# Two PSUM banks of the common ring per attention unit, in place of one ring bank and a third of a shared bank

## The chip, the cores and the metric

The kernel runs on one core of one Trainium2 chip. The metric is the device time of one execution in microseconds (us), the median of several runs. Five engines work side by side, each on its own list of instructions in order: TensorE (PE in the profile; its weight loads are listed as PEld), VectorE (DVE), ScalarE (ACT), GpSimd (POOL) and SyncE (SP), which here only issues DMAs. PE writes its products into PSUM, which this kernel divides into eight banks of 512 fp32 columns by 128 partitions; DVE and ACT read them from there.

## The reference

Two layers over 2048 tokens of width 1024. What matters here is group B, attention with 8 query heads of width 64 and 2 key/value heads:

```python
for l in range(DEPTH):                      # DEPTH = 2
    h = rmsnorm(x, pre_g[l])
    u_a, v_a, g_a, q, k, v, g_b = jnp.split(h @ w_in[l], idx, axis=-1)
    y_a = gmlp_group(u_a, v_a, ...) * silu(g_a)
    y_b = gqa_axial_attention(q, k, v, ...) * silu(g_b)   # softmax(q k^T) v, all 2048 keys
    x = x + rmsnorm(concat(y_a, y_b) @ w_out[l], post_g[l])
```

## The kernel before

**Stages.** Each layer has a projection stage (`Project.run`, the products with `w_in`, the gating of group A, the rotary embedding) and an attention stage (`attend`). In the profiled execution attention takes about 617 to 1372 us in the first layer and 1981 to 2726 us in the second.

**Units and steps.** Attention is cut into 32 units per layer, `units[u]`: one query head and one block of 512 queries, which are four pieces of 128 (`TPG` = 4). The loop at L1097 walks over steps `k`; a unit has 16 steps, one for each 128 keys. A step does, in this order: on PE two matmuls for the scores `sp` of its 128 keys against the 512 queries (L1106, L1107); on ACT two exponentials of them, an fp16 one into `p_hi` (called `p_parts` in the profile) and an fp32 one into `p_f`; on POOL, and on DVE in 15% of the steps, the difference `p_lo` of the two (also `p_parts`). Then come the jobs that a table `later` holds for this step: for most steps one `pmax` matmul on PE with a row maximum `mx` on DVE, which prepare a later unit; then some matmuls `pout` of the output projection that fill in (`pop_fill`). Last, PE multiplies the probabilities of the step three back (`LAG` = 3) with the values.

**The product with the values.** For each of the four query pieces j there are two matmuls into `s.av[j]` (L1137, L1139): `p_hi` with 129 columns (64 of the value's low part, 64 of its high part, one column of ones for the denominator) and `p_lo` with the last 65 of these. The eight matmuls of a step add to the same 4 x 129 columns over all 16 steps. 4 x 129 = 516 columns are more than one bank's 512. So pieces 0 to 2 lie in a bank `po` from the common ring (`ps_t`, L73, seven banks), and piece 3 in one third of a fixed eighth bank `po_3` (L165), `u % 3` saying which third.

**The end of a unit.** After a unit's last step, `finish` (L722) enters its closing jobs into `later`. In the following step, `evac`: for each of the two banks an ACT copy of the low parts to `o_pair` and a small DVE operation that makes `rden` of the denominators. One step later, `add`: for each bank a DVE addition of the high parts. Then, another step later, `gate` and `mul` (DVE), and after every second unit a transposition (`trans`, `split`). Since the jobs of `later` stand ahead of the product with the values within a step, a unit's `evac` is recorded just ahead of the first product of the next unit, and its `add` ahead of the second one.

**What sets the order.** The operations of this stage are recorded through `Pinned` (L86), which keeps each engine's instructions in the order in which the program writes them. The framework that builds the program adds the waits: it orders any two accesses to one bank of one tile by different engines, whichever columns they touch. It also deals out the ring: a new tile gets a bank whose previous tile is finished, and its first writer waits for the last reader of that previous tile. All other PSUM tiles (`sp`, `pmax`, `pout`, `t2`, `py`, and in projection `pp`, `pt`, `sq`) come from the same ring.

Of the kernel before, what the change touches and what calls it, by code (L numbers as in the profile page):

```python
# [9 lines left out]
F32 = mybir.dt.float32  # L10
# [9 lines left out]
P = 128  # L20
D = 1024
ND = D // P
GRP = 512
TPG = GRP // P
# [6 lines left out]
VN = 2 * HD + 1  # L31
# [9 lines left out]
def encoder(ctx: ExitStack, tc, x, w_in, w_out, pre_g, post_g, ln_a_g, ln_a_b,  # L41
# [16 lines left out]
    psum = ctx.enter_context(tc.tile_pool(name="psum", bufs=1, space=PSUM))  # L58
# [8 lines left out]
    def f_t(name, n=GRP, dt=F32):  # L67
        return fp.tile([P, n], dt, name=name, tag="f")
# [2 lines left out]
        return rowp.tile(list(shape), dt, name=name, tag="row")  # L71

    def ps_t(name):  # L73
        return psum.tile([P, GRP], F32, name=name, tag="ps", bufs=7)

    class Pinned:

# [66 lines left out]
    class Background:  # L144
# [16 lines left out]
        def flush(self):  # L161
            while self.jobs:
                self.jobs.pop(0)[1]()

    po_3 = psum.tile([P, GRP], F32, name="po_3")  # L165

    bg = Background()
    PASSES = ((0, 0), (0, 1), (1, 0))
# [467 lines left out]
    T_DELAY = 9  # L636
    VA_DELAY = 9
    LAG = 3
    AV_BANKED = 3
    N_HI = 8  # L640
    N_F = 4
    N_LO = 8
# [4 lines left out]
    def attend(l, kv, nxt):  # L647

        k_st, k_lo, _, v16 = kv
# [23 lines left out]
        def at(k, f):  # L673
            later.setdefault(k, []).append(f)
# [47 lines left out]
        def finish(u, k):  # L722

            qb, h = units[u]
            side = h % 2
            s, pr = state[u], pairs[u // 2]
            r = slice(side * HD, (side + 1) * HD)

            def evac():
                if side == 0:  # L730
                    pr.o = f_t("o_pair").rearrange("p (t e) -> p t e", t=TPG)
                s.rd = small.tile([P, TPG], F32, name="rden")
                for b, js in s.banks:
                    ACT.copy(pr.o[:, js, r], b[:, :, 0:HD])
                    DVE.tensor_scalar(s.rd[:, js], b[:, :, 2 * HD], layers[l].two, None, ALU.mult)

            def add():
                for b, js in s.banks:
                    DVE.tensor_tensor(pr.o[:, js, r], b[:, :, HD:2 * HD], pr.o[:, js, r], ALU.add)

            def gate():
                DVE.reciprocal(s.rd, s.rd)
                gv = pr.gb[:, :, r]
                DVE.tensor_tensor(gv, gv, s.rd.unsqueeze(2).broadcast_to([P, TPG, HD]), ALU.mult)

            def mul():
                DVE.tensor_tensor(pr.o[:, :, r], pr.o[:, :, r], pr.gb[:, :, r], ALU.mult)

            def trans():
                pr.py = ps_t("py")  # L750
                for j in range(TPG):
                    PE.transpose(pr.py[:, j * P:(j + 1) * P], pr.o[:, j], ident)

            def split():
                y_hi = f_t("y_hi", dt=F32R)
                y_lo = f_t("y_lo", dt=F32R)
                ACT.copy(y_hi, pr.py)
                DVE.tensor_tensor(y_lo, pr.py, y_hi.bitcast(F32), ALU.subtract)
                if (qb, h) == units[-1]:
                    last_y.extend([y_hi, y_lo])  # L760
                    return
                c = 4 + h // 2
                nc.sync.dma_start(y_d[qb][:, c, 0], y_hi.bitcast(F32))
                nc.sync.dma_start(y_d[qb][:, c, 1], y_lo.bitcast(F32))

            if u + 1 == len(units):
                for n, f in ((0, evac), (0, add), (1, gate), (1, mul), (2, trans), (2, split)):
                    at(k + n, f)
                return
            at(k, evac)  # L770
            at(k + 1, add)
            at(k + 2, gate)
            at(k + 3, mul)
            if side == 0:
                return
            at(k + 5, trans)
            at(k + 6, split)
# [257 lines left out]
        def p_hi(k):  # L1035
            return his[k % N_HI]

        def p_f(k):
            return fs[:, k % N_F]

        def p_lo(k):
            return los[k % N_LO]
# [15 lines left out]
        def load_gb(u):  # L1058
            qb, h = units[u]
            pairs[u // 2].gb = f_t("gb").rearrange("p (t e) -> p t e", t=TPG)  # L1060
            nc.sync.dma_start(pairs[u // 2].gb, gb_d[qb][:, :, (h // 2) * P:(h // 2 + 1) * P])

        def pop_fill(n):
            for _ in range(n):
                if fill and fill[0] is None:
                    if not last_y:
                        return
                    fill.pop(0)
                if fill:
                    fill.pop(0)()  # L1070

        def weight(k):
            return 2 if k >= total - 2 * NT else 1
# [3 lines left out]
        def sub_lo(k, engine):  # L1077
            engine.tensor_tensor(p_lo(k), p_f(k), p_hi(k), ALU.subtract)

        def dve_share(k):  # L1080

            n = SHARE_0 if k < NH * NT else SHARE
            return k * n // 100 != (k + 1) * n // 100
# [13 lines left out]
        for k in range(end + 4):  # L1097
            if k < total:
                u, i = k // NT, k % NT
                s = state[u]  # L1100
                kv = units[u][1] // (NH // NKV)
                if i == 0 and units[u][1] % 2 == 0:
                    load_gb(u)
                ss = slice(i * P, (i + 1) * P)
                sp = ps_t("sp")
                PE.matmul(sp, k_st[:, kv, ss], s.qs, start=True, stop=False)  # L1106
                PE.matmul(sp, k_lo[0:HD + 2, kv, ss], s.q2[0:HD + 2], start=False, stop=True)  # L1107
                ACT.activation(p_hi(k), sp, AF.Exp)
                ACT.activation(p_f(k), sp, AF.Exp)
                if not dve_share(k):  # L1110
                    sub_lo(k, POOL)
            if post_queue:
                post_queue.pop(0)()
            kb = k - 1
            if 0 <= kb < total and dve_share(kb):
                sub_lo(kb, DVE)
            for f in later.pop(k, []):
                f()
            if k >= end:
                pop_fill((4, 5, 20)[min(k - end, 2)])  # L1120
            elif fill:
                room = sum(weight(q) for q in range(k, max(k + 1, fill_to)))
                pop_fill(-(-len(fill) * weight(k) // room))
            kb = k - LAG
            if 0 <= kb < total:
                u, i = kb // NT, kb % NT
                s = state[u]
                kv = units[u][1] // (NH // NKV)
                if i == 0:
                    po = ps_t("po")[:, 0:AV_BANKED * VN].rearrange("p (t e) -> p t e", e=VN)  # L1130
                    p3 = po_3[:, u % 3 * VN:(u % 3 + 1) * VN].rearrange("p (t e) -> p t e", e=VN)
                    s.banks = [(po, slice(0, AV_BANKED)), (p3, slice(AV_BANKED, TPG))]
                    s.av = [po[:, j] for j in range(AV_BANKED)] + [p3[:, 0]]
                for j in range(TPG):
                    js = slice(j * P, (j + 1) * P)
                    first = i == 0 and j in (0, AV_BANKED)
                    PE.matmul(s.av[j], p_hi(kb)[:, js], v16[:, i, kv, 0:VN], start=first, stop=False,  # L1137
                              skip_group_check=True)
                    PE.matmul(s.av[j][:, HD:VN], p_lo(kb)[:, js], v16[:, i, kv, HD:VN], start=False,  # L1139
                              stop=i == NT - 1, skip_group_check=True)  # L1140
                if i == NT - 1:
                    finish(u, k + 1)
                    if units[u][1] == NH - 1 and u + 1 < len(units):
                        fill_to = min(k + 16 + NH * NT, total - LAST_0)
                        at(k + 16, lambda qb=units[u][0]: fill.extend(out_steps(qb)))
# [7 lines left out]
        n = 0  # L1153
# [23 lines left out]
    for l in range(DEPTH):  # L1177
        k_t = big_t([P, 2, NKV, S], "k_t", F16)
        kv = [k_t[:, 0], k_t[:, 1]]
        v_t = big_t([P, 2, NT * NKV * HD], "v_st")  # L1180
        kv.append(v_t.bitcast(F32)[:, 0].rearrange("p (t k d) -> p t k d", t=NT, k=NKV))
        v_h = v_t.bitcast(F16).rearrange("p a n -> p (a n)")[:, 4 * NT * NKV * HD - NT * NKV * VW:]
        kv.append(v_h.rearrange("p (t k d) -> p t k d", t=NT, k=NKV))
        att = attend(l, kv, layers[l + 1] if l + 1 < DEPTH else None)
        layers[l].run(kv, layers[l].first, *next(att))
        for _ in att:
            pass
# [40 lines left out]
```

## Time and profile before

| | us |
|---|---|
| median of 3 runs | 2754.39 (2753.72 to 2756.24) |
| the profiled execution, its own time | 2757.03 |
| span of the profiled execution, first to last instruction | 2755.3 |
| PE busy in it | 2585.4 |
| DVE / ACT / POOL busy in it | 1840.4 / 1527.0 / 1250.9 |

The span starts with the first instruction, so 1.7 us of the profiled execution's time lie around it. The mean granted PE clock over the span is 0.986 of full speed. A busy time is the union of an engine's instructions; a matmul's row lasts from its start to the modelled end of its results, and the next one may start before that, so a row's length is not the distance between two starts. The idle time given for a group is the time just ahead of its instructions in which the engine had nothing running, with the name of what ended it. Nearly all rows of the attention stage carry L86, the line of the recording helper, so they are told apart by the names of their tiles.

### The profile page before, as it was taken

To read this page: it belongs to the slowest core of one execution; us is meant where nothing else is said; L and a number is where in the kernel's file an instruction comes from. 1 tells how busy PE (TensorE), PEld (TensorE's weight loads), DVE (VectorE), ACT (ScalarE), POOL (GpSimd) and SP (SyncE) were. 2 spreads that over 40 slices of the span, in tenths; PEclk is the share of its full clock that TensorE was granted. 3 is DMA by queue.
4 is the path that set the end of the run, shared out by engine and by line. 5 is a ranking of instruction groups with operands and counts; after the bars stand their busy time and mean duration, and the time that the engine had idled before them with its cause. 6 is when DMAs were issued, how large, how long until landed. Compare 5 with 4: busy or idle time off the path is not lost.

```text
span 2755.3 us, 53763 instructions
## 1 busy us (share of the span) xinstructions
PE 2585.4 (94%) x20794; PEld 1943.9 (71%) x20794; DVE 1840.4 (67%) x3973; ACT 1527.0 (55%) x3087; POOL 1250.9 (45%) x1049
## 2 busy tenths in 40 slices
PE   7999999998889989999999999999988999999997
PEld 7998999765556556556699989997655565555555
DVE  7762888875666666666497538887766566566655
ACT  5221422118877777787743224221388878778774
POOL 1210221017676666676632111210266767667665
PEclk9999999999999999999999999999999999999999
DMA  4534423323131222222354434232312312321303
GB/s 136 151 100 121 153 82 85 101 75 104 65 94 46 95 84 81 81 81 73 111 189 139 120 110 144 79 115 76 115 57 72 89 61 72 90 73 53 102 34 138
DMA packets 275192, 265.13 MB, mean 96 GB/s; under 512 B 19188, under 2 KB 233332, under 8 KB 274936
## 3 DMA queue, kind: packets, MB, share of 16 engines
q1 hardware_dynamic: 274936, 261.70, 30.6%
q8 instruction: 163, 2.67, 0.4%
q14 instruction: 93, 0.76, 0.1%
HBM read 176.57 MB, written 85.07 MB: 95 GB/s over the span
## 4 chain that ended last, share of the span: by engine, by line
PE 72%; DVE 13%; ACT 8%; issue 3%; DMA 2%; POOL 1%; SPq 0%; DVEq 0%; POOLq 0%; ACTq 0%
PE pp L86 26%; PE sp L86 14%; PE po L86 11%; PE pout L86 11%; PE pmax L86 7%; ACT p_f L86 3%; ACT p_parts L86 3%; PE pt L86 3%; DVE fc L367 2%; DVE mx L86 2%; DVE w_lo L272 1%; DVE o_pair L86 1%; DVE o_t L86 1%; DMA fa<-in_rope_dram 1%; DVE rden L86 1%
## 5 line engine op out<-in xcount | busy, mean ns | idle before, releaser
L86 POOL TENSOR_TENSOR p_parts<-p_f,p_parts 128x512 f16<-128x512 f32 x872 | 1029.7, 1192 | 460.1 <-ACT p_f L86 373.4
L86 ACT ACTIVATE p_parts<-sp 128x512 f16<-128x512 f32 x1024 | 621.2, 607 | 313.3 <-PE sp L86 310.8
L86 PEld LDWEIGHTS <-p_parts 128*128 128x128 f16 x8192 | 406.2, 98 | 408.0 <-issue 358.2
L86 DVE TENSOR_REDUCE mx<-pmax 128x1 f32<-128x512 f32 x768 | 519.7, 685 | 254.5 <-PE pmax L86 252.0
L86 PE MATMUL po<-v_st,p_parts 128*128 128x129 f16 (+1 forms) x8192 | 561.0, 209 | 120.2 <-DVE rden L86 71.5
L86 PE MATMUL pout<-wo,y_t 128*128 128x512 f32 x1488 | 665.8, 511 | 1.5 <-DVE mx L86 1.5
L86 ACT ACTIVATE p_f<-sp 128x512 f32<-128x512 f32 x1024 | 619.4, 605 | 0.0
L86 PE MATMUL pp<-w_hi,hT 128*128 128x256 f32 x3584 | 496.6, 287 | 2.3 <-DVE k_t L400 1.3
L86 PEld LDWEIGHTS pp<-w_hi,hT 128*128 128x128 f32 x3584 | 457.2, 192 | 6.9 <-DVE k_t L400 1.8
L86 PE MATMUL sp<-q,k_t 66*128 66x512 f16 x1024 | 396.2, 387 | 0.0
L86 PE MATMUL pmax<-k_t,q_m 128*128 128x512 f16 x1024 | 393.6, 386 | 1.7 <-DVE fb L452 1.3
L86 PE MATMUL sp<-q_st,k_t 128*128 128x512 f16 x1024 | 394.1, 385 | 0.0
L86 PEld LDWEIGHTS pout<-wo,y_t 128*128 128x128 f32 x1488 | 283.8, 192 | 123.4 <-issue 6.6
L472 POOL TENSOR_TENSOR fl<-fa,fh 128x512 fp32r<-128x512 f32 x32 | 42.8, 1336 | 539.8 <-ACT fh L471 495.7
L86 PE MATMUL pp<-hT,w_hi 128*128 128x512 f32 x1024 | 273.1, 413 | 0.0
L86 PE MATMUL pp<-w_lo,hT 128*128 128x256 f32 x1792 | 261.3, 289 | 0.6 <-DVE w_lo L272 0.6
L86 PEld LDWEIGHTS pp<-w_lo,hT 128*128 128x128 f32 x1792 | 233.9, 193 | 1.8 <-DVE w_lo L272 0.8
L86 PEld LDWEIGHTS pp<-hT,w_hi 128*128 128x128 f32 x1024 | 192.8, 189 | 35.2
L701 DVE TENSOR_REDUCE mx<-pmax 128x1 f32<-128x512 f32 x256 | 172.6, 687 | 49.0 <-PE pmax L86 47.5
L86 PEld LDWEIGHTS <-q_m 128*128 128x128 f16 x1024 | 100.7, 99 | 144.5 <-issue 47.0
L271 ACT CAST w_hi<-w_raw 128x1024 fp32r<-128x1024 f32 (+1 forms) x92 | 89.6, 1013 | 124.7 <-PE pp L86 93.1
L86 DVE TENSOR_TENSOR p_parts<-p_f,p_parts 128x512 f16<-128x512 f32 x152 | 113.1, 744 | 41.8 <-ACT p_f L86 41.5
(156 smaller groups left out, 2518.5 us busy)
## 6 DMA issues: line engine op xcount, KB each, us to landing
w_raw<-in_w_in_dram SPq DMA_DIRECT2D x28, 1024.0 KB
y_t<-y_d SPq DMA_DIRECT2D x56, 512.0 KB
w_raw<-in_w_in_dram SPq DMA_DIRECT2D x32, 512.0 KB
x_t<-in_x_dram SPq DMA_DIRECT2D x16, 512.0 KB
z_d<-fb SPq DMA_DIRECT2D x32, 256.0 KB
gb_d<-fa SPq DMA_DIRECT2D x32, 256.0 KB
fb<-z_d SPq DMA_DIRECT2D x32, 256.0 KB
y_d<-fh SPq DMA_DIRECT2D x32, 256.0 KB
```

What stands on the lines that cost most here:

```text
L86: return tc.keep_in_program_order(call(*args, **kw))
L271: nc.scalar.copy(hi[:, sl], raw[:, sl])
L272: nc.vector.tensor_tensor(lo[:, sl], raw[:, sl], hi.bitcast(F32)[:, sl], ALU.subtract)
L367: nc.vector.tensor_tensor(t2[:, :, :, lo:lo + 16], qn[:, :, :, hi:hi + 16], tbi[:, :, 1:2, lo:lo + 16].broadcast_to([P, 2, n, 16]), ALU.mult)
L472: nc.gpsimd.tensor_tensor(lo, th, hi.bitcast(F32), ALU.subtract)
L701: dve.tensor_reduce(s.mx[:, j, c:c + 1], ps, AX.X, ALU.max)
```

## The change

The ring gets all eight banks (`bufs=8`), and the fixed bank `po_3` is gone. A unit takes two banks `po` from the ring, each for two query pieces (258 columns). The matmul that opens a bank is now that of the pieces 0 and 2. `add` is no longer a job of its own: the additions are written into `evac`, behind each bank's copy and `rden`, and so one step earlier than before. The number of ACT copies, `rden` operations and additions per unit stays at two each; their shapes change from 3 + 1 to 2 + 2 pieces.

```diff
     def ps_t(name):
-        return psum.tile([P, GRP], F32, name=name, tag="ps", bufs=7)
+        return psum.tile([P, GRP], F32, name=name, tag="ps", bufs=8)
...
-    po_3 = psum.tile([P, GRP], F32, name="po_3")
...
-    AV_BANKED = 3
...
                 for b, js in s.banks:
                     ACT.copy(pr.o[:, js, r], b[:, :, 0:HD])
                     DVE.tensor_scalar(s.rd[:, js], b[:, :, 2 * HD], layers[l].two, None, ALU.mult)
-
-            def add():
-                for b, js in s.banks:
                     DVE.tensor_tensor(pr.o[:, js, r], b[:, :, HD:2 * HD], pr.o[:, js, r], ALU.add)
...
             at(k, evac)
-            at(k + 1, add)
             at(k + 2, gate)
...
                 if i == 0:
-                    po = ps_t("po")[:, 0:AV_BANKED * VN].rearrange("p (t e) -> p t e", e=VN)
-                    p3 = po_3[:, u % 3 * VN:(u % 3 + 1) * VN].rearrange("p (t e) -> p t e", e=VN)
-                    s.banks = [(po, slice(0, AV_BANKED)), (p3, slice(AV_BANKED, TPG))]
-                    s.av = [po[:, j] for j in range(AV_BANKED)] + [p3[:, 0]]
+                    s.banks = []
+                    for b in range(2):
+                        po = ps_t("po")[:, 0:2 * VN].rearrange("p (t e) -> p t e", e=VN)
+                        s.banks.append((po, slice(2 * b, 2 * b + 2)))
+                    s.av = [po[:, t] for po, _ in s.banks for t in range(2)]
                 for j in range(TPG):
                     js = slice(j * P, (j + 1) * P)
-                    first = i == 0 and j in (0, AV_BANKED)
+                    first = i == 0 and j % 2 == 0
```

PE's instructions stand in the same order in both programs, with the same shapes; what differs is where the products go and for what they wait. The rows below are PE's, in the first product of the second unit with the values and up to the scores of the next step, before the change (`p_parts_6801` holds the `p_hi` tiles, `p_parts_6802` the `p_lo` tiles; a name in brackets is the engine whose progress the instruction waits for):

```order
L86 MATMUL po_7137<-v_st_254,p_parts_6801 128x129
L86 LDWEIGHTS p_parts_6802
L86 MATMUL po_7137<-v_st_254,p_parts_6802 128x65
L86 LDWEIGHTS p_parts_6801
L86 MATMUL po_3_137<-v_st_254,p_parts_6801 128x129 [waits DVE_49]
L86 LDWEIGHTS p_parts_6802
L86 MATMUL po_3_137<-v_st_254,p_parts_6802 128x65
L86 LDWEIGHTS k_t_253
L86 MATMUL sp_7146<-q_st_6895,k_t_253 128x512
```

The same place on PE with the change:

```order
L86 LDWEIGHTS p_parts_6800
L86 MATMUL po_7140<-v_st_253,p_parts_6800 128x129 [waits Activation_49]
L86 LDWEIGHTS p_parts_6801
L86 MATMUL po_7140<-v_st_253,p_parts_6801 128x65
L86 LDWEIGHTS p_parts_6800
L86 MATMUL po_7140<-v_st_253,p_parts_6800 128x129
L86 LDWEIGHTS p_parts_6801
L86 MATMUL po_7140<-v_st_253,p_parts_6801 128x65
L86 LDWEIGHTS k_t_252
L86 MATMUL sp_7149<-q_st_6895,k_t_252 128x512 [waits DVE_49]
```

The wait for DVE in front of piece 3, in the bank that all units share, is gone; the second new bank is opened by piece 2 with a wait for ACT, the last reader of whatever tile had that bank before, and the next `sp` has a wait that it did not have.

DVE around the end of the second unit, before the change:

```order
L86 TENSOR_REDUCE mx_7009<-pmax_7442 128x1 [waits PE_49]
L86 TENSOR_SCALAR rden_7445<-po_7137,two_v_257 128x3 [waits Activation_49]
L86 TENSOR_SCALAR rden_7445<-po_3_137,two_v_257 128x1 [waits Activation_49]
L86 TENSOR_TENSOR wo_6805<-wo_raw_7466,wo_6804 128x512 [waits DMAHW4_49,Activation_49]
L86 TENSOR_REDUCE mx_7009<-pmax_7470 128x1 [waits PE_49]
L86 TENSOR_TENSOR o_pair_7130<-po_7137,o_pair_7130 128x3x64
L86 TENSOR_TENSOR o_pair_7130<-po_3_137,o_pair_7130 128x64
L86 TENSOR_REDUCE mx_7009<-pmax_7490 128x1 [waits PE_49]
```

The same place on DVE with the change:

```order
L86 TENSOR_REDUCE mx_7009<-pmax_7443 128x1 [waits PE_49]
L86 TENSOR_SCALAR rden_7446<-po_7139,two_v_256 128x2 [waits Activation_49]
L86 TENSOR_TENSOR o_pair_7130<-po_7139,o_pair_7130 128x2x64
L86 TENSOR_SCALAR rden_7446<-po_7140,two_v_256 128x2 [waits Activation_49]
L86 TENSOR_TENSOR o_pair_7130<-po_7140,o_pair_7130 128x2x64
L86 TENSOR_TENSOR wo_6804<-wo_raw_7470,wo_6803 128x512 [waits DMAHW4_49,Activation_49]
L86 TENSOR_REDUCE mx_7009<-pmax_7474 128x1 [waits PE_49]
L86 TENSOR_REDUCE mx_7009<-pmax_7492 128x1 [waits PE_49]
```

The additions have moved ahead of the weight preparation `wo` (which comes in eight steps of a layer) and ahead of the row maximum of the next step; the row maximum that stood ahead of `rden` still does.

More of the change, by code (lines that the diff above doesn't have):

```diff
@@ L766, in finish @@
             if u + 1 == len(units):
-                for n, f in ((0, evac), (0, add), (1, gate), (1, mul), (2, trans), (2, split)):
+                for n, f in ((0, evac), (1, gate), (1, mul), (2, trans), (2, split)):
                     at(k + n, f)
```

## The prediction

> **What bounds the kernel now.** I read the table of stages first, to see which engine is full where, then PE's waits, then the timeline of one unit's end, then the granted clock in short windows. The windows give PE, PEld, DVE, ACT and POOL busy us, the granted clock, the DMA share and GB/s:
>
> ```profile
> 0.00:617.00 617.00, 593.64 (x4041) 532.13 (x4042) 450.63 (x1041) 175.10 (x335) 101.23 (x77) 0.99 0.37 112
> 1396.00:1980.00 584.00, 578.24 (x3990) 520.82 (x3989) 431.47 (x961) 157.37 (x291) 99.53 (x75) 1.00 0.37 110
> 626.00:1372.00 746.00, 683.62 (x6214) 427.64 (x6212) 466.11 (x967) 587.34 (x1213) 509.63 (x430) 0.97 0.25 81
> 1987.00:2726.00 739.00, 682.28 (x6279) 428.64 (x6276) 443.45 (x889) 579.56 (x1183) 510.52 (x434) 0.99 0.25 80
> ```
>
> The first two rows are projection, the last two attention. PE is the fullest engine in all four. In attention it stands idle for 62.4 and 56.7 us, and ACT, the next, is busy for 79% and 78%. Nearly all of that idle time has one place, in front of the product with the values (group of PE rows; then the waits of the whole execution: total, times, longest):
>
> ```profile
> L86 PE MATMUL po<-v_st,p_parts 128*128 128x129 f16 (+1 forms) x8192 | 561.0, 209 | 120.2 <-DVE rden L86 71.5 <-DVE o_pair L86 38.2 <-DVE p_parts L86 5.4
> PE po L86 <- DVE rden L86: 71.5, 62, 2.0
> PE po L86 <- DVE o_pair L86: 38.2, 47, 3.2
> ```
>
> 62 is one for each unit's beginning but the first of each layer. The timeline of one such place (start, us, engine; a bracket gives the idle time before):
>
> ```profile
> 1067.15 0.38 PE L86 MATMUL sp<-q_st,k_t 128*128 128x512 f16 x1
> ...
> 1068.28 0.44 PE L86 MATMUL po<-v_st,p_parts 128*128 128x129 f16 x6
> 1068.28 0.59 ACT L86 ACTIVATE p_f<-sp 128x512 f32<-128x512 f32 x1
> ...
> 1068.76 0.45 ACT L86 COPY o_pair<-po 128x192 f32<-128x192 f32 x2
> ...
> 1069.12 0.34 DVE L86 TENSOR_SCALAR rden<-po,two_v 128x3 f32<-128x3 f32 x2 [0.17 <-ACT o_pair L86]
> ...
> 1069.52 0.25 PE L86 MATMUL po<-v_st,p_parts 128*128 128x129 f16 x2 [0.80 <-DVE rden L86]
> ...
> 1069.60 0.38 PE L86 MATMUL sp<-q_st,k_t 128*128 128x512 f16 x1
> ...
> 1070.45 0.69 DVE L86 TENSOR_REDUCE mx<-pmax 128x1 f32<-128x512 f32 x1 [0.87 <-PE pmax L86]
> ...
> 1070.72 0.44 PE L86 MATMUL po<-v_st,p_parts 128*128 128x129 f16 x6
> ...
> 1071.06 0.48 DVE L86 TENSOR_TENSOR o_pair<-po,o_pair 128x192 f32<-128x192 f32 x2
> ...
> 1071.59 0.25 PE L86 MATMUL po<-v_st,p_parts 128*128 128x129 f16 x2 [0.44 <-DVE o_pair L86]
> ...
> 1071.68 0.38 PE L86 MATMUL sp<-q_st,k_t 128*128 128x512 f16 x1
> ...
> 1072.59 0.52 PE L86 MATMUL po<-v_st,p_parts 128*128 128x129 f16 x8
> ...
> 1072.95 0.38 PE L86 MATMUL sp<-q_st,k_t 128*128 128x512 f16 x1
> ```
>
> Six of eight matmuls run; the seventh, piece 3, is the first into `po_3`. There it waits for the chain `sp`, two exponentials, two copies, two `rden` of the unit before, though these read other columns. In the next step it waits again, for the additions, which stand on DVE behind a row maximum that itself waits for this step's `pmax`. In the third step all eight run.
>
> **Term 1, the idle time at `po_3`.** 71.5 + 38.2 = 109.7 us. With the change each unit's banks are its own, so a new unit's product waits for nothing of the old unit. These waits cannot stay: in the built program no product of a unit names a reader of the unit before.
>
> **Term 2, the tails of the rows.** An idle time is counted from the modelled end of the row before, but the next matmul would have started earlier. An undisturbed group of eight takes 1072.95 - 1072.59 = 0.36 us to the next `sp`. The first stalled one takes 1069.60 - 1068.28 = 1.32, so 0.96 is lost where the row says 0.80; the second loses 1071.68 - 1070.72 - 0.36 = 0.60 where it says 0.44. That is 0.16 more each time: (62 + 47) x 0.16 = 17.4 us.
>
> **Term 3, the clock.** Spells of half clock follow stalls. Window before, then the spell; then the same stretch of work in both layers (units 7 and 8, once with such a spell, once without):
>
> ```profile
> 779.50:782.90 3.40, 1.69 (x19) 1.00 (x16) 1.78 (x6) 1.94 (x6) 2.19 (x3) 1.00 0.00 0
> 782.90:786.30 3.40, 3.40 (x18) 1.83 (x15) 2.02 (x3) 1.18 (x3) 1.95 (x2) 0.50 0.02 5
> 774.80:796.10 21.30, 19.59 (x186) 11.63 (x183) 11.99 (x24) 16.82 (x36) 14.91 (x14) 0.92 0.24 79
> 2137.00:2156.70 19.70, 17.99 (x187) 10.90 (x184) 11.32 (x24) 16.87 (x37) 15.12 (x14) 1.00 0.25 79
> 796.10:816.30 20.20, 17.73 (x183) 11.21 (x180) 13.44 (x27) 16.61 (x36) 14.88 (x14) 0.92 0.10 33
> 2156.70:2175.40 18.70, 16.23 (x182) 10.48 (x179) 13.33 (x26) 16.50 (x36) 14.96 (x14) 1.00 0.10 34
> ```
>
> A window of 3.4 us with PE half idle (1.69 busy) is followed by 3.4 us at 0.50. Such a spell makes the same work 21.30 - 19.70 = 1.6 and 20.20 - 18.70 = 1.5 us longer, about nine tenths of the 1.7 us of lost clock. The stretches of attention with spells:
>
> ```profile
> 626.00:826.00 200.00, 177.15 (x1669) 107.69 (x1668) 122.20 (x225) 161.70 (x331) 141.67 (x122) 0.94 0.27 83
> 826.00:976.00 150.00, 140.94 (x1240) 88.36 (x1239) 94.85 (x211) 115.05 (x240) 98.64 (x83) 0.97 0.21 69
> 976.00:996.00 20.00, 16.73 (x139) 9.88 (x138) 13.71 (x18) 13.06 (x27) 11.18 (x11) 0.83 0.16 53
> 2020.00:2110.00 90.00, 77.36 (x716) 46.84 (x714) 54.41 (x98) 70.54 (x144) 59.63 (x53) 0.94 0.21 67
> 2170.00:2200.00 30.00, 27.99 (x254) 17.53 (x251) 16.69 (x31) 22.95 (x47) 21.62 (x20) 0.94 0.47 133
> 2340.00:2360.00 20.00, 18.08 (x160) 10.90 (x159) 10.84 (x22) 14.87 (x31) 12.78 (x12) 0.91 0.01 1
> ```
>
> Lost clock is length times what is missing to 1: 12.0 + 4.5 + 5.4 + 1.8 + 1.8 = 25.5 us, without the third row, whose spell begins in a wait for `p_parts` that the change does not touch:
>
> ```profile
> 982.13 0.73 PE L86 MATMUL po<-v_st,p_parts 128*128 128x65 f16 x7 [3.27 <-DVE p_parts L86]
> ```
>
>  Nine tenths of the 25.5 are 23; I take 21, because some spells lie partly on waits that term 1 counts already. By the Trainium skill, TensorE: Matmul & The Clock Gate, section HAM oscillation, the clock drops only after PE idles for about 3.4 us; the stalls here are at most 3.2 us and mostly near 1, so by that rule the spells would have another cause and this term would be 0. The rows speak for the share of a window instead.
>
> **Term 4, what the new order costs.** Copies, `rden` and additions stay two per unit. A copy of three pieces and one of one piece lasted 347 and 265 ns, the additions 348 and 216:
>
> ```profile
> L86 ACT COPY o_pair<-po 128x192 f32<-128x192 f32 x64 | 22.2, 347 | 11.7 <-PE po L86 11.7
> L86 ACT COPY o_pair<-po 128x64 f32<-128x64 f32 x64 | 17.0, 265 | 0.0
> L86 DVE TENSOR_TENSOR o_pair<-po,o_pair 128x192 f32<-128x192 f32 x64 | 22.3, 348 | 0.0
> L86 DVE TENSOR_TENSOR o_pair<-po,o_pair 128x64 f32<-128x64 f32 x64 | 13.8, 216 | 0.4
> ```
>
> Two equal ones should lie halfway (estimates: 306 and 282 ns), so both engines have the same work. DVE already stopped for ACT's copies before its two `rden`; now it does so with the additions in between. Behind them wait the weight preparation `wo`, the next row maximum and, on PE, whoever wants that `pmax` bank. What can be late is a bank. While old and new pair overlap, four of eight banks are left for scores, maxima and `pout`; before there were five of seven. In the new build the first bank of an old pair is written again two steps after the step with `evac` at the earliest, the second three steps after it in nearly all units. Laid out on the timeline above: without the stalls the step after `evac` begins at 1068.64, the next at 1070.1, the one after at 1071.5. The copies end by 1069.3 (1068.76 + 0.45 and a little), the first addition by about 1069.6, the second by 1070.0. So 0.9 us are to spare for a `pmax` 0.4 us into the step at 1070.1, and 1.5 us for the `sp` at 1071.5. In the shortest units (18.70 us less 2.47 idle over 16 steps, 1.0 us a step) nothing is to spare; there are a handful of them. Scores and maxima, too, now follow each other more closely in a bank, at a unit's start by one step instead of two. These units (7 and 8 of each layer) also come near a second bound: ACT starts an exponential every 0.48 us when it has no wait (1068.28 to 1068.76 above), so 32 of them and the copies take 15.8 us of a unit in which PE works 16.2, and POOL 15.0. In the long units, of 20 to 25 us, ACT has room.
>
> Bounds: -3 us (the eighth bank also serves projection, where PE idles 23.4 and 5.8 us, mostly at the start) and +41 us (0.66 us at each of the 62 boundaries, the size of half the old pair of stalls of 71.5/62 = 1.15 and 0.16). The nearest row is the third step above, eight matmuls without a wait, so I take a value near the lower end: 15 us, a quarter of a microsecond for each boundary.
>
> **The sum.** 2757.0 (the profiled execution: span 2755.3 and 1.7 around it) - 109.7 - 17.4 - 21 + 15 = 2623.9. That execution is 2.6 us above the median of the runs, 2754.39, so the forecast for the median is **2621 us**.
>
> **The rivals.**
> - *The ring becomes the wait.* With four banks left, a stall like today's second one (38.2/47 = 0.81 us, and 0.16 of tail) stays at every boundary: 62 x 0.97 = 60 instead of 15, and about 10 us of the spells stay: 2621 + 45 + 10 = 2676. For it: the closer reuse. Against it: the layout above, and that neither `sp` nor `pmax` waits for a bank today, with five left:
>
> ```profile
> L86 PE MATMUL pmax<-k_t,q_m 128*128 128x512 f16 x1024 | 393.6, 386 | 1.7 <-DVE fb L452 1.3
> L86 PE MATMUL sp<-q_st,k_t 128*128 128x512 f16 x1024 | 394.1, 385 | 0.0
> ```
>
> - *The spells stay.* If the clock depends on something else than these stalls, term 3 is 0: 2621 + 21 = 2642. Against it: every spell I looked at stands behind a half-idle window, and the twin rows without spell have the same stalls with another position in the window's grid. By the rule of the Trainium skill, TensorE: Matmul & The Clock Gate, section HAM oscillation, it would come out this way.
> - *Slower than before.* The additions are held behind copies that are behind exponentials; if ACT lags by a whole step and more, PE meets the old pair's banks before they are free, and stalls with `sp` for the full chain. It begins to cost when ACT runs over 0.9 us late at a boundary, and outweighs the gain when it is 133/62 = 2.1 us later still; at 3 us of stall per boundary the time is 2621 + 186 - 15 = 2792. ACT is busy for 587 of 746 us, and would be for 587 of some 680, so it should not run that late.
> - *It does not do what it says*: the new pair waits for the old one through the ring after all; 2754. The build speaks against it.
>
> **How the numbers follow.** Forecast 0.70, ring 0.13, spells 0.11, slower 0.04, no change 0.02. The range goes from 2602 (new waits at their lower bound, 2621 - 18 = 2603) to 2662: it holds the spells' rival, the upper bound of the new waits just about (2621 + 26 = 2647, with some spells back), and leaves out the ring at full price. A measurement of this kernel tells about 0.2% (5.5 us) from no change. Faster by more than that: 0.70 + 0.13 + 0.11 = 0.94; within: 0.02; slower: 0.04.
>
> **What would show it.** In the profile after: no row of `po` waiting for `rden` or `o_pair`; PE busy above 97% of the attention windows; a clock near 1.00 in them, with one spell left near the `p_parts` wait of the first layer. The forecast is wrong if `sp` or `pmax` rows show new idle time behind `o_pair` or `p_f` of more than 30 us in all, if the spells stay, or if ACT becomes busy without a gap.

## The result, and the profile after

| | before | after |
|---|---|---|
| median, us | 2755.31 (2753.72 to 2757.38, 4 runs) | **2626.11** (2623.41 to 2627.27, 4 runs) |
| profiled execution, us | 2757.03 | 2623.41 |
| its span, us | 2755.3 | 2621.5 |
| mean granted PE clock | 0.986 | 0.996 |

The ratio is 0.9529, with a 95% interval from 0.9513 to 0.9546. The forecast for the median was 2621 us, with a range from 2602 to 2662; the measured median is 5 us above the forecast. The sum for the profiled execution was 2623.9.

The attention stages of both layers after the change, without their first two microseconds (PE, PEld, DVE, ACT, POOL busy us with instructions, granted clock, DMA share, GB/s):

```profile
624.00:1301.00 677.00, 663.35 (x6221) 416.57 (x6219) 467.93 (x967) 583.38 (x1213) 514.61 (x431) 1.00 0.29 90
1917.00:2590.00 673.00, 665.05 (x6242) 418.86 (x6241) 442.60 (x887) 573.37 (x1177) 509.75 (x431) 1.00 0.27 86
```

PE is busy for 98.0% and 98.8% of these stretches, and idle for 13.7 and 8.0 us where it was for 62.4 and 56.7. ACT now takes 86% and 85% of the time; PE is still the bound. PE's groups in this stage (busy us, mean ns; idle time before them and its releasers):

```profile
L86 PE MATMUL po<-v_st,p_parts 128*128 128x129 f16 (+1 forms) x8192 | 538.4, 208 | 12.7 <-DVE p_parts L86 7.5 <-POOL p_parts L86 4.0
...
L86 PE MATMUL sp<-q_st,k_t 128*128 128x512 f16 x1024 | 389.7, 381 | 0.9 <-DVE o_pair L86 0.4
L86 PE MATMUL pmax<-k_t,q_m 128*128 128x512 f16 x1024 | 389.6, 382 | 3.6 <-DVE mx L86 1.4 <-ACT p_f L86 1.1 <-DMA q_m<-q_d 0.7
...
L86 PE MATMUL py<-ident,o_pair 128*128 128x128 f32 x128 | 19.8, 277 | 7.0 <-DVE o_pair L86 3.1 <-ACT o_t L86 3.0 <-ACT p_f L86 0.5
```

The 120.2 us in front of `po` are 12.7, and neither `rden` nor `o_pair` is among what it waits for. What is left there are the probabilities themselves. The scores and maxima, which take their banks from the ring, wait for 4.5 us in all. The transposition `py`, which waited for 1.0 us, now waits for 7.0.

The timeline at the beginning of a unit, in the 1.5 us that begin with the first `sp` below and end with the last (start, us, engine):

```profile
1017.62 0.38 PE L86 MATMUL sp<-q_st,k_t 128*128 128x512 f16 x1
1017.74 0.44 ACT L86 COPY o_pair<-po 128x128 f32<-128x128 f32 x2
...
1018.05 0.22 DVE L86 TENSOR_SCALAR rden<-po,two_v 128x2 f32<-128x2 f32 x1
...
1018.18 0.28 DVE L86 TENSOR_TENSOR o_pair<-po,o_pair 128x128 f32<-128x128 f32 x1
...
1018.51 0.28 DVE L86 TENSOR_TENSOR o_pair<-po,o_pair 128x128 f32<-128x128 f32 x1
...
1018.74 0.52 PE L86 MATMUL po<-v_st,p_parts 128*128 128x129 f16 x8
1019.10 0.38 PE L86 MATMUL sp<-q_st,k_t 128*128 128x512 f16 x1
```

The old unit's copies, `rden` and additions run beside PE as they did, but all eight matmuls of the new unit's first product run in one group, and the next `sp` starts 0.36 us after them: the distance that the prediction took from an undisturbed step.

Where the 133.6 us between the two profiled executions went follows from the distances between the `sp` rows that begin the steps, added up over the 64 units of both layers. The two attention stages became 130.2 us shorter (1491.1 to 1360.9), the two projections 3.4 us (1227.0 to 1223.6). Within attention, before minus after, by step of a unit:

```
step    0    1    2    3     4     5    6    7    8     9     10   11   12   13   14   15
us      0.4  0    0    79.2  44.0  9.9  5.2  0.3  -9.0  -3.5  1.2  1.1  1.3  0.1  0.1  0
```

Steps 3 and 4 are those with the two stalls. The start of the seventh matmul, in these steps of all units, lay 128.0 us later than an undisturbed one before, and 0.2 us after. Steps 5 and 6, in which nothing was stalled, are 15.1 us shorter as well; steps 8 and 9 are 12.5 us longer. Over the attention stages that is 127.8 for the stalls, 12.5 given back in steps 8 and 9, and by subtraction 14.9 for the rest. This rest is not the clock alone: steps 3 and 4 became only 123.2 us shorter, so some of the 127.8 was given back there at once. The part on the prediction takes the two apart.

### The profile page after: what moved, and what is told of

Same layout as the page of the kernel before. It is cut to its first block, busy times and chain, and to the rows that moved or that the text cites. A ratio compares the mean times of both kernels' runs of the same rounds, so it can differ in the third digit from the quotient of the medians.

```text
span 2621.5 us, 53877 instructions
## 1 busy us (share of the span) xinstructions
PE 2551.2 (97%) x20794; PEld 1924.5 (73%) x20794; DVE 1845.0 (70%) x3973; ACT 1519.8 (58%) x3087; POOL 1256.5 (48%) x1049
## 4 chain that ended last, share of the span: by engine, by line
PE 80%; DVE 10%; ACT 4%; issue 2%; DMA 2%; POOL 1%; SPq 0%; DVEq 0%; POOLq 0%; ACTq 0%
PE pp L86 29%; PE sp L86 14%; PE pout L86 12%; PE po L86 12%; PE pmax L86 8%; PE pt L86 3%; DVE fc L365 2%; ACT p_f L86 1%; ACT p_parts L86 1%; DVE o_t L86 1%; DVE w_lo L270 1%; DVE mx L86 1%; PE py L86 1%; DMA fa<-in_rope_dram 1%; POOL p_parts L86 1%
## 5 line engine op out<-in xcount | busy, mean ns | idle before, releaser
L86 PE MATMUL pout<-wo,y_t 128*128 128x512 f32 x1488 | 657.2, 505 | 1.8 <-DVE mx L86 1.8
L86 PEld LDWEIGHTS <-p_parts 128*128 128x128 f16 x8192 | 395.1, 98 | 286.4 <-issue 233.8
L86 PE MATMUL po<-v_st,p_parts 128*128 128x129 f16 (+1 forms) x8192 | 538.4, 208 | 12.7 <-DVE p_parts L86 7.5
L86 PE MATMUL sp<-q,k_t 66*128 66x512 f16 x1024 | 390.9, 382 | 0.0
```

What stands on the lines that cost most here:

```text
L86: return tc.keep_in_program_order(call(*args, **kw))
```

## The experiments

Three questions were open. Does the gain come from the units no longer sharing a bank (theory S), from the additions that now come a step earlier (R1), or does it need the larger ring and equal halves (R2)? Do the stalls cause the spells of half clock, and by which measure of idle time? And what took 12.5 us back in steps 8 and 9?

### The additions early, the banks as before (e1_adds_early)

The kernel before, with the additions written into `evac`:

```diff
                     DVE.tensor_scalar(s.rd[:, js], b[:, :, 2 * HD], layers[l].two, None, ALU.mult)
-
-            def add():
-                for b, js in s.banks:
                     DVE.tensor_tensor(pr.o[:, js, r], b[:, :, HD:2 * HD], pr.o[:, js, r], ALU.add)
...
-            at(k + 1, add)
```

> The kernel before with one part of the change: the additions are written into the job with the copies, one step earlier; banks as before (ring of seven and the bank that all units share). Theory S (the gain comes from units no longer sharing a bank): the first wait at a unit's start gets longer by the additions in the chain, about 1.15 + 0.4 us at 62 places (96 us of idle time behind o_pair, none behind rden), the second wait (38.2 us) and 47 tails go, some of the half-clock spells go: about 2724 us (2705 to 2745). Rival R1 (the earlier additions give most of the gain): 2626 to 2660 us.

It took 2738.88 us (ratio 0.9931, 0.9915 to 0.9948). PE's longest row of waits (total us, times, longest):

```profile
PE po L86 <- DVE o_pair L86: 96.8, 62, 2.4
```

The second stall is gone, and the first one has become longer by the additions: 62 waits with a total of 96.8 us in place of 71.5 and 38.2. The early additions alone give some 19 us, 0.69% of the time, out of the 4.71% that the change gives, so R1 falls. The time is above the centre that S expected, and inside its range; most of the half clock stayed, 44.4 us of it in the attention stages where the kernel before had 58.0.

### The banks new, the additions late (e2_adds_late)

The changed kernel, with `add` a job of its own again, one step after `evac`:

```diff
+
+            def add():
+                for b, js in s.banks:
                     DVE.tensor_tensor(pr.o[:, js, r], b[:, :, HD:2 * HD], pr.o[:, js, r], ALU.add)
...
             at(k, evac)
+            at(k + 1, add)
             at(k + 2, gate)
```

> The changed kernel with the additions one step later again, as before the change; two ring banks per unit stay. Theory S: no product with the values waits for rden or o_pair; the old pair of banks is held for one step longer, so up to 10 us of new waits for a bank: 2626 to 2637 us. Rival R1 (the earlier additions give most of it): the second wait of 38.2 us and its tails come back, 2670 us or more.

It took 2632.86 us (ratio 0.955, 0.9535 to 0.9564), and no row of `po` waits for `rden` or `o_pair`. What it has more than the changed kernel stands in front of the scores and the maxima:

```profile
L86 PE MATMUL pmax<-k_t,q_m 128*128 128x512 f16 x1024 | 389.4, 382 | 4.9 <-ACT p_f L86 2.6 <-DVE mx L86 1.7 <-DMA q_m<-q_d 0.3
L86 PE MATMUL sp<-q_st,k_t 128*128 128x512 f16 x1024 | 389.2, 380 | 9.0 <-DVE o_t L86 4.4 <-DVE o_pair L86 2.0 <-ACT p_f L86 1.0
```

The banks alone bring nearly the whole gain. With the banks separate, the early additions are worth some 6 us more (ratios 0.955 and 0.9529, whose intervals just overlap); by the traces, attention is 9.7 us shorter with them.

### Two fixed banks, 3 + 1 pieces, a ring of six (e3_two_fixed)

The kernel before; piece 3 of a unit goes to one of two fixed banks in turn, which the ring gives up:

```diff
-        return psum.tile([P, GRP], F32, name=name, tag="ps", bufs=7)
+        return psum.tile([P, GRP], F32, name=name, tag="ps", bufs=6)
...
-    po_3 = psum.tile([P, GRP], F32, name="po_3")
+    po_3 = [psum.tile([P, GRP], F32, name=f"po_3_{n}") for n in range(2)]
...
-                    p3 = po_3[:, u % 3 * VN:(u % 3 + 1) * VN].rearrange("p (t e) -> p t e", e=VN)
+                    p3 = po_3[u % 2][:, 0:VN].rearrange("p (t e) -> p t e", e=VN)
```

> The kernel before with two fixed banks for the fourth piece, taken in turn by the units, and a ring of six; three pieces in a ring bank and the place of the additions as before. Theory S: neighbours share no bank, so the waits for rden and o_pair go, and with them the half-clock spells; a ring of six costs up to 15 us: 2626 to 2645 us. Rival R2 (the gain needs the larger ring or two equal halves): 2700 us or more.

It took 2672.01 us (ratio 0.9695, 0.9679 to 0.9711), between the two expectations. PE's groups of the three products:

```profile
L86 PE MATMUL po<-v_st,p_parts 128*128 128x129 f16 (+1 forms) x8192 | 537.3, 208 | 7.6 <-DVE p_parts L86 3.9 <-POOL p_parts L86 2.6 <-DVE o_t L86 0.5
...
L86 PE MATMUL sp<-q_st,k_t 128*128 128x512 f16 x1024 | 389.9, 381 | 9.5 <-DVE o_t L86 4.8 <-ACT p_f L86 2.8 <-ACT m_rows L86 1.0
L86 PE MATMUL pmax<-k_t,q_m 128*128 128x512 f16 x1024 | 389.7, 382 | 13.8 <-DVE mx L86 6.3 <-ACT p_f L86 5.7 <-DVE o_t L86 1.1
```

The stalls at the seventh matmul are gone here too (0.1 us), with unequal halves, late additions and a smaller ring: separate banks are enough, as S has it. What was missed is the price of the ring: against the changed kernel, attention is 27.3 us longer, the projections 19.8 and the tail 2.1. The late additions are part of the 27.3, since they cost 9.7 in e2; how much they cost with these banks was not measured. The 15 us expected for the ring were too few: the projections alone lose more.

### The changed kernel with a ring of seven (e4_ring7)

```diff
-        return psum.tile([P, GRP], F32, name=name, tag="ps", bufs=8)
+        return psum.tile([P, GRP], F32, name=name, tag="ps", bufs=7)
```

> The changed kernel with a ring of seven, one PSUM bank left unused: while two pairs overlap, three banks are left for scores, maxima and pout instead of four. If the ring was near its limit (the rival of the prediction), PE now waits for banks at each unit's start: 0.5 to 1.5 us at 62 places, 2660 to 2720 us, and half-clock spells come back with it. If the ring has slack: 2626 to 2635 us. I expect about 2670.

It took 2664.49 us (ratio 0.9666, 0.9651 to 0.968). The waits that it adds (total us, times, longest):

```profile
PE sp L86 <- ACT p_f L86: 6.0, 16, 0.6
...
PE pmax L86 <- DVE mx L86: 5.2, 7, 1.7
...
PE pmax L86 <- ACT p_f L86: 4.1, 14, 0.6
...
PE sp L86 <- DVE mx L86: 3.6, 18, 0.3
```

Here the ring is a wait, in many small pieces. By the starts of PE's rows, `sp`, `pmax` and `pout`, which all take their banks from the ring, come 44.6 us later in all than with eight banks, and `po` and `py` 7.2 us sooner. Attention is 36.7 us longer than with eight banks: 15.7 of it in step 3, where old and new pair overlap and three banks are left for the rest, and the remainder spread over a unit's other steps, where five are left. The kernel before and the changed one both leave six there; e3, which leaves five too, also loses in steps with no overlap: in steps 1, 2, 10 and 14 together 10.4 us against the changed kernel, where e4 loses 9.1. The spells of half clock expected with such waits did not come back (3 spells, 20.5 us within the span). So the eighth bank carries a part of the gain: without it some 38 us of the 129 are given up. Projection is 4.5 us longer with seven banks, which is enough to explain the 3.4 us that the change gained there.

### The old wait put back without a shared bank (e5_wait_rden)

The changed kernel; in the first product of a unit, behind piece 2, a small transposition on PE reads the old unit's `rden` and writes a tile that nobody reads:

```diff
+                    if i == 0 and u > 0 and j == 2:
+                        PE.transpose(ps_t("t2")[0:TPG, 0:P], state[u - 1].rd, ident)
```

> The changed kernel with one more PE instruction per unit: behind the third piece of a unit's first product PE transposes rden of the unit before (4 x 128, result unused), so it waits for copies and rden in the place where it waited before the change, without any shared bank. Stall about 1.15 + 0.15 us of idle time and 0.16 of tail, the transposition 0.12: 62 x 1.6 = 98 us, 2725 us. Clock by the share of a window: a stall of 1.3 us is less than half of 3.4, so few spells or none. Clock by gaps of 3.4 us: none either.

It took 2713.65 us (two runs, 2709.84 and 2717.47; ratio 0.9836, 0.9775 to 0.9897):

```profile
PE t L86 <- DVE rden L86: 80.9, 62, 2.1
```

A wait of PE for the old unit's `rden`, with nothing shared, brings back 98.1 us of delay at this place, the transposition itself included, and some 85 us of time (0.9836 - 0.9529 of 2757); in the profiled execution attention is 95.0 us longer than in the changed kernel. Only the first of the two old waits is put back, so the time of the kernel before is not reached. The median is 11 us below the 2725 us expected. There are 10 spells of half clock (47.9 us) where the changed kernel has 4 (24.3 us).

### The same wait made three times as long (e6_wait_long)

As e5, but the transposition reads a copy of `rden` that went through six small DVE operations in a row:

```diff
+                s.chain = small.tile([P, TPG], F32, name="chain")
+                DVE.tensor_scalar(s.chain, s.rd, 1.0, None, ALU.mult)
+                for _ in range(5):
+                    DVE.tensor_scalar(s.chain, s.chain, 1.0, None, ALU.mult)
...
-                        PE.transpose(ps_t("t2")[0:TPG, 0:P], state[u - 1].rd, ident)
+                        PE.transpose(ps_t("t2")[0:TPG, 0:P], state[u - 1].chain, ident)
```

> As the one before, but PE waits for a chain of six small DVE operations behind the last addition: a stall of about 2.8 us of idle time per unit, always shorter than 3.4. Without half-clock spells 2626 + 62 x (2.8 + 0.16 + 0.12) = 2817 us. If the clock halves after a window in which PE is half idle: a stall of 2.8 us fills half of a window of 3.4 in about 8 of 10 positions, some 50 spells of 3.4 us at 0.5, 1.55 us each: about 2895 us. If it takes a gap of about 3.4 us: no spells, 2817 us.

It took 2907.23 us (ratio 1.0537, 1.0492 to 1.0583), with 66 spells of half clock (263.7 us) and a mean clock of 0.955. Its waits, then the timeline of one, then the clock's window in which it falls and the next:

```profile
PE t L86 <- DVE chain L86: 164.8, 57, 3.9
PE t L86 <- DVE rs_o L86: 13.7, 5, 3.0
```

```profile
712.47 0.37 PE L86 MATMUL t<-ident,chain 128*4 128x128 f32 x1 [2.98 <-DVE chain L86]
```

```profile
708.88:712.29 3.41, 0.61 (x8) 0.34 (x6) 3.24 (x13) 1.91 (x6) 1.15 (x1) 1.00 0.66 211
712.29:715.70 3.41, 3.23 (x17) 1.86 (x17) 1.46 (x4) 1.09 (x2) 0.64 (x1) 0.50 0.24 96
```

The 62 waits have a mean of (164.8 + 13.7) / 62 = 2.9 us, and a wait of 2.98 us is followed by a window at half clock. Only 5 of the 62 are longer than 3.4 us, and yet there are 66 spells, 63 of them in the attention stages. The time without spells was put at 2817 us, with them at 2895. So gaps clearly shorter than 3.4 us lower the clock of this kernel. The rule of the Trainium skill, TensorE: Matmul & The Clock Gate, section HAM oscillation, to have no idle gaps of PE above about 3.4 us, is too lenient here: 57 of the 62 gaps keep it. The Trainium skill, TensorE: Matmul & The Clock Gate, section A second HAM failure mode: psum-queue depth-cycling, tells of a kernel whose clock oscillates because PE is idle for short times between groups of matmuls; the 66 spells behind waits of 2.9 us in the mean agree with that.

### The transposition two steps later (e7_trans_late), and the changed kernel again (e8_again)

What PE waits for in steps 8 and 9 of the changed kernel shows in its timeline (the bracket gives the idle time before; `gate` makes `gb`, `mul` the `o_pair` from it):

```profile
778.17 1.04 DVE L86 TENSOR_TENSOR gb<-gb,rden 128x256 f32<-128x256 f32 x1
...
779.14 0.68 DVE L86 TENSOR_TENSOR p_parts<-p_f,p_parts 128x512 f16<-128x512 f32 x1
...
779.73 0.38 PE L86 MATMUL pmax<-k_t,q_m 128*128 128x512 f16 x1
779.74 1.37 DVE L86 TENSOR_TENSOR o_pair<-o_pair,gb 128x256 f32<-128x256 f32 x1
...
781.17 0.66 PE L86 MATMUL py<-ident,o_pair 128*128 128x128 f32 x4 [1.06 <-DVE o_pair L86]
```

PE has started its last matmul 1.44 us before and waits for DVE's product `o_pair`, which it transposes. It is the unit's own closing work, on DVE behind a `p_parts` of the running unit; with the stalls gone PE gets there sooner. By the starts of PE's rows in steps 8 and 9, `py` comes 7.3 us later in all than in the kernel before, the matmuls behind a late `p_parts` 3.5 us, `pmax` 1.8 us. The edit:

```diff
-            at(k + 5, trans)
-            at(k + 6, split)
+            at(k + 7, trans)
+            at(k + 8, split)
```

> The changed kernel with the transposition of a unit pair and its split two steps later (steps 10 and 11 of the next unit instead of 8 and 9). In the changed kernel PE idles 7.1 us in front of py, in 9 of 32 places, because without the old stalls it reaches the transposition before DVE and ACT have caught up. If that is where part of the gain is given back, these waits go and the time falls by 7 us and some tails: about 2617 us, 8 us below the changed kernel on the same chip. If the wait only moves to another place, 2626 us.

> The changed kernel once more, beside the one with the later transposition on the same chip: 2626 us, between 2622 and 2629.

On one chip, e7 took 2619.84 us (2618.13 to 2621.07; ratio 0.9498, 0.9485 to 0.9511) and the changed kernel 2624.48 us (2622.58 to 2627.99; ratio 0.952, 0.9507 to 0.9533). The row of `py` in e7:

```profile
L86 PE MATMUL py<-ident,o_pair 128*128 128x128 f32 x128 | 19.5, 275 | 2.7 <-DVE mx L86 2.7
```

The wait for `o_pair` is gone, and 2.7 us have come in front of the new place, ended by a row maximum. The gain is 4.6 us, not 8: the idle time in front of `py` fell from 7.0 to 2.7, that is by 4.3, and did not vanish. The runs of the two do not overlap, the intervals of the ratios do by a little. It confirms that this wait was a part of what was given back, and e7 is the fastest of these kernels.

## Why the prediction was right

**Term 1 and term 2, the idle time at `po_3` and the tails.** Together 127.1 us; the starts of the seventh matmuls measure 127.8. The two idle rows had only 109.7 of these, so the tail of 0.16 us for each stall, read off two places, was needed. e2 and e3 show that separate banks alone remove it, e5 that the wait alone, without any shared bank, costs most of it again, and e1 that the early additions are not the cause.

**Term 3, the clock.** Mechanism and size were both right. By the clock's records, half clock fell from 80.0 us (16 spells, some of them two windows long) to 24.3 us (4 spells), and within the attention stages from 58.0 to 6.8 us. What that is worth shows where no stall lay. PE's rows stand in the same order in both profiled executions, so the steps can be compared one by one. Outside steps 3, 4, 8 and 9, 739 steps have no half clock in either execution, and together they differ by 1.0 us. In 24 steps there were 41.5 us of half clock before and none after; these are 19.5 us shorter, 0.47 us for each us at half clock, close to the 1.5 / 3.4 = 0.45 of the twin stretches. Eight of the stalled steps 4 held another 12.1 us of half clock. They became 13.8 us shorter, only 1.9 us more than their stalls measure: 6.4 us of this half clock fell inside the stalls, where PE was waiting. For such spells the prediction had taken off a little, from 23 to 21 us; 19.5 + 1.9 = 21.4 were found. The rival that the spells stay has fallen with e6 and with the clock after.

"One spell left near the `p_parts` wait of the first layer" was wrong. The wait is there, but no spell follows it. The wait, and the windows of the clock around it:

```profile
938.62 0.47 PE L86 MATMUL po<-v_st,p_parts 128*128 128x65 f16 x7 [3.26 <-DVE p_parts L86]
```

```profile
933.70:937.10 3.40, 1.66 (x15) 0.91 (x13) 3.40 (x4) 2.88 (x7) 2.64 (x3) 1.00 0.09 24
937.10:940.50 3.40, 1.88 (x21) 1.26 (x22) 3.40 (x5) 0.94 (x2) 0.92 (x1) 1.00 0.78 257
940.50:943.90 3.40, 3.40 (x36) 2.05 (x34) 2.23 (x4) 2.92 (x7) 3.00 (x3) 1.00 0.15 57
```

The wait of 3.26 us is as long as the 3.27 us before, but it falls across two windows, which are idle for 1.74 and 1.52 us (1.69 and 1.57 where the windows are laid exactly by the clock's records), and the clock stays at 1.00. In e7 the same wait, 3.26 us again, falls into one window, idle for 3.41 - 0.23 = 3.18 us, and half clock follows:

```profile
933.90:937.31 3.41, 0.23 (x2) 0.09 (x1) 3.41 (x4) 1.61 (x5) 2.44 (x3) 1.00 0.21 83
937.31:940.73 3.42, 3.33 (x21) 2.00 (x22) 2.52 (x5) 1.08 (x2) 0.50 (x1) 0.50 0.74 224
```

So whether this wait brings a spell hangs on where the windows lie; in e8, the changed kernel on the same chip as e7, it is split over two windows again, idle for 1.60 and 1.67 us, and no spell follows. The spells that remain lie at the start of the kernel, at the first microseconds of both attention stages, and in the tail.

**Term 4, what the new order costs.** 15 us were taken. 12.5 us were measured in steps 8 and 9, and some 6 more hide in steps 3 and 4: without those that held half clock, 62 steps 3 lost stalls of 81.7 us and became 79.3 us shorter, and 54 steps 4 lost 34.2 and became 30.5 us shorter. Together that is 18.6, so the size was 3.6 us too low, and most of the place was wrong. "What can be late is a bank" holds for `pmax` in step 4, which starts 2.7 us later in all, partly behind ACT's `p_f`; in front of `sp` and `pmax` there are 4.5 us of idle time, from all causes. The larger part is PE waiting for other engines' results, `py` and the probabilities, at a point five steps further on. The two estimated durations were right; the groups by shape show 303 and 280 ns against 306 and 282:

```profile
L86 ACT COPY o_pair<-po 128x128 f32<-128x128 f32 x128 | 29.5, 303 | 11.5 <-PE po L86 11.5
```

```profile
L86 DVE TENSOR_TENSOR o_pair<-po,o_pair 128x128 f32<-128x128 f32 x128 | 35.9, 280 | 0.0
```

The layout of the bank reuse was right in its margins: e4, with a bank fewer at the overlap, loses 15.7 us at exactly that step. The rival "the ring becomes the wait" is thus real, but one bank away.

**Not in the sum.** Projection became 3.4 us shorter, which the prediction had as a bound of term 4 (3 us) and not as a term; the 4.5 us that e4 loses there suggest that it is the eighth bank's. So the sum, 2623.9 against 2623.4, agrees better than its terms do: 3.6 us too little for the new waits and 3.4 us of projection left out cancel. A part of the agreement is luck of the runs, too: the profiled execution before lies 2.6 us above its median and the one after is the fastest of its four. By medians the gain is 129.2 us (2755.31 - 2626.11), where the forecast stands for 133.4 (2754.39 - 2621).

## What to carry to other kernels

In this program a PSUM bank shared by successive accumulations ties the new one to the last reader of the old one, whichever columns they use; give successive accumulations banks of their own before looking for anything finer. Price such a stall from start to start of the matmuls, not by the idle time, and count how many banks are left for everything else, in a unit's middle and at the overlap, since one bank fewer took back some 38 of 129 us here. When a long stall goes, look a few steps on for the next result that the freed engine needs: moving that consumer later was worth another 4.6 us.

## What the runs showed of the hardware

In these runs the clock goes by windows of about 3.41 us on a grid that is fixed within an execution: in the changed kernel the stretches between one change of the granted clock and the next last 1, 1, 174, 1, 378, 1 and 203 of them. What decides, as far as these runs go, is how long PE is idle within a window, not how long a gap is; the wait of 3.26 us, with a spell in e7 and without one in the changed kernel, shows it. In the attention stages of before, after, e1, e2, e4, e5 and e6, taken window by window, and of the windows that themselves ran at full clock, the least idle one that was followed by half clock had from 1.64 us (e1) to 2.66 us (e4) of idle time, and the most idle one that was not from 1.38 (e2) to 1.78 us (before): a limit near 1.7 us, half a window. The two ranges overlap by 0.14 us, and the ends of PE's rows are modelled, so the limit is not known more closely. A window that ran at half clock was followed by another one with less idle time, 0.92 us in before and 0.64 us in e6. In e3, two spells came behind windows with only 1.41 and 1.52 us idle; these stay open. A window just past the limit, in the changed kernel ahead of its first attention stage, and the one behind it:

```profile
616.20:619.60 3.40, 1.59 (x11) 0.60 (x10) 2.43 (x5) 3.33 (x7) 2.58 (x3) 1.00 0.34 128
619.60:623.00 3.40, 3.40 (x25) 2.03 (x23) 0.10 (x1) 2.82 (x7) 3.40 (x4) 0.50 0.75 214
```

3.40 - 1.59 = 1.81 us idle, and the next window runs at 0.50 although PE is busy throughout.
